# The first norm's modulation weights in four parts instead of two, and the tokens at the head of the load queue

## The chip, the cores and the metric

The kernel runs on one core of one Trainium2 chip. The metric is the device time of one execution in microseconds (us), the median of three runs. A core has five engines that run side by side and meet through semaphores: TensorE (PE in the profile, with its weight loads shown apart as PEld), VectorE (DVE), ScalarE (ACT), GpSimd (POOL) and SyncE (SP), which here issues nearly all loads. Each engine takes its own instructions in their order.

## The reference, cut to what matters

One block of a diffusion backbone over 512 latent tokens (x) with 256 context tokens (ctx), 1024 features, float32. Only its beginning is touched by the change:

```
mod_lat = jnp.split(jax.nn.silu(c) @ w_ada[l] + b_ada[l], 6, axis=-1)
mod_ctx = jnp.split(jax.nn.silu(c_ctx)[None, :] @ w_ada[l] + b_ada[l], 6, axis=-1)
sh1, sc1, gt1, sh2, sc2, gt2 = mod_lat
...
pl = project(modulate(rmsnorm(x, g_mix[l]), sh1, sc1), w_in[l], w_dec_up[l], b_dec[l])
pc = project(modulate(rmsnorm(ctx, g_mix[l]), sh1c, sc1c), w_in[l], w_dec_up[l], b_dec[l])
```

The first norm needs a shift and a scale for each feature, from the first 2 x 1024 columns of `w_ada` (8.4 MB). `project` multiplies the modulated tokens by `w_in`; attention, convolution, gates and the channel layer (SwiGLU) follow, and are the same in both kernels.

## The kernel before, in words

Tokens are kept turned, features on the partitions: `h[f]` is feature tile f (128 features x 512 tokens) of the modulated tokens, f = 0 to 7. float32 operands are split into a high and a low half, and a product takes three matmuls (`mm3`: high x high, high x low, low x high).

**Loads.** SP issues the loads in program order: `c_rows` (c and c_ctx, 4 KB each, L167), `vrow` (norm gains and `b_ada`, L180), the four token tiles `xt` (512 KB each, L236), the first half of `w_ada` (`wa`, 8 loads of 512 KB: for each input tile k the 512 shift and 512 scale columns of feature tiles 0 to 3, L272), head 0's weights for input tiles 0 to 3 (`r_w`: two units of two tiles, 557 KB each in four loads, L438), the second half of `w_ada` (16 loads of 256 KB, L266), the other two units of `r_w`, then small vectors and two context tiles. An operand `w_dec_up` (`wraw`) comes over POOL.

**Before the first product.** ACT applies Silu to the turned `c_rows` (`c`), DVE puts the result into `cw`. Each token tile is squared and summed on ACT (`junk`), scaled on DVE (`normed`), turned by PE (`xtp`), and copied into `xsT` by ACT and DVE (`turn`). `ada_rows` multiplies `cw` into `wa` on PE; DVE copies the rows (`adar`); `mod_cols` turns them with a selecting matrix `sel` on PE (`adac`), and DVE adds `b_ada` (`modT`) and the gain (`gs`). `modulate(f)` makes `h[f]`: ACT the high half, DVE the low half (`xsT` in place, then a subtraction). `w0_split` splits a unit of `r_w` into `h_w` (ACT) and `l_w` (DVE).

**Gather.** For k = 0 to 7, `gather_v` multiplies `h[k]` into four banks `v` (12 matmuls), `gather_kq` into `kl` and `q` (3 matmuls each). `ada_rows(1)`, `mod_cols(1)` and the remaining modulates are written at k = 3. After k = 5 the context tiles are turned (`xtp` again) and modulated (`hc`, `mod_ctx`). Then the same gather runs over the context (`v`, `kc` from `hc`), and at its k = 5 PE turns `st` (`ddt`), which ACT and DVE make from the finished `v` banks in `v_done`, after `hc`. `warm` gives PE products of zeros.

From there on PE, DVE, ACT and SP have the same instructions in the same order in both kernels; between the helpers `act_`, `dve`, `mm` and `tr` the written order is kept.

Of the kernel before, what the change touches and what calls it, by code (L numbers as in the profile page):

```python
# [8 lines left out]
F32 = mybir.dt.float32  # L9
# [33 lines left out]
R_GM, R_GF, R_BA, R_GH, R_BD, R_WC, R_N = 0, 8, 16, 64, 66, 74, 98  # L43
# [3 lines left out]
def hybrid_block(ctx: ExitStack, tc: tile.TileContext, x, c, ctxt, c_ctx, w_ada, b_ada, g_mix, w_in,  # L47
                 w_dec_up, b_dec, g_head, w_gla_out, w_conv, w_conv_out, w_mix_out, g_ffn,
                 w_ffn_in, w_ffn_out, g_final, out):
    nc = tc.nc  # L50
    x, ctxt, out = x[0], ctxt[0], out[0]
    w_ada, w_in, w_gla_out, w_conv_out, w_mix_out = (w[0] for w in (w_ada, w_in, w_gla_out, w_conv_out, w_mix_out))
# [3 lines left out]
    wp = ctx.enter_context(tc.tile_pool(name="wp", bufs=3))  # L56
# [8 lines left out]
    def u2(name, dt=F32, shape=(P, 512)):  # L65
        return up.tile(list(shape), dt, tag="u2", name=name, bufs=NU)
# [126 lines left out]
    for d in range(2):  # L193
# [4 lines left out]
        s = 1 if d == 0 else -1  # L198
# [9 lines left out]
    for d in range(2):  # L208
        t = cst.tile([P, NT, P], F32, name=f"TP{d}")
# [7 lines left out]
    root = sm.tile([P, 1], F32, tag="ss", name="root")  # L217
    nc.scalar.activation(root, c2[:, 0:1], AF.Sqrt, bias=eps, scale=0.0)
    c2v = c2.rearrange("p (s k) -> p k s", s=2)
    hp = tc.alloc_tile_pool(name="hp", bufs=1)  # L220

    cw = u2("cw", F32, (P, KT, 32))
    nc.vector.memset(cw, 0.0)
    nc.vector.tensor_copy(cw[:, :, 0:2], c2v)

    sel = hp.tile([P, 2, 2], F32, name="sel")
    for s_ in range(2):
        nc.vector.tensor_add(sel[:, s_, :], ident[:, 32 * s_:32 * s_ + 2], ident[:, 64 + 32 * s_:66 + 32 * s_])
# [4 lines left out]
    def token_load(i):
        if i < NT:
            xt = hp.tile([P, D], F32, tag="xt", name=f"xt{i}", bufs=4)
            nc.sync.dma_start(xt, x[i * P:(i + 1) * P, :])  # L236
        else:
            xt = wp.tile([P, D], F32, tag="raw", name=f"xt{i}", bufs=4)
            nc.sync.dma_start(xt, ctxt[(i - NT) * P:(i - NT + 1) * P, :])
        return xt  # L240
# [14 lines left out]
    modT = cst.tile([P, KT, 2, 2], F32, name="modT")  # L255
    gs = cst.tile([P, KT, 2], F32, name="gs")

    def ada_load(hf):

        us = []  # L260
        for k in range(KT):
            src = w_ada[k * P:(k + 1) * P, :2 * D].rearrange("p (s f) -> p s f", s=2)[:, :, hf * 512:(hf + 1) * 512]
            if hf == 1:
                ts = [(uo if s_ else uh)(f"wa{k}{s_}") for s_ in range(2)]
                for s_ in range(2):
                    nc.sync.dma_start(ts[s_], src[:, s_, :])  # L266
            else:
                if k % 2 == 0:
                    t = wp.tile([P, 2, 512], F32, tag="raw", name=f"wa0{k}", bufs=4)
                else:  # L270
                    t = hp.tile([P, 2, 512], F32, tag="wa", name=f"wa0{k}", bufs=4)
                nc.sync.dma_start(t, src)  # L272
                ts = [t[:, s_, :] for s_ in range(2)]
            us.append(ts)
        return us

    def ada_rows(hf, us):

        rows = gbank(f"ada{hf}")
        for k in range(KT):  # L280
            for s_ in range(2):
                g_ = 64 * (k % 2) + 32 * s_
                mm(rows[g_:g_ + 32, :], cw[:, k, :], us[k][s_], start=k < 2, stop=k >= KT - 2)
        rsb = u2(f"adar{hf}")
        dve.tensor_copy(rsb, rows)
        return rsb

# [7 lines left out]
        dve.tensor_scalar(src, src, g_, sh, ALU.mult, ALU.add)  # L295
        dve.tensor_sub(lo, src, f32(hi))

    def mod_cols(hf, rsb):
        cp = gbank(f"adac{hf}")
        for i in range(4):  # L300
            mm(cp[:, 4 * i:4 * i + 4], rsb[:, i * P:(i + 1) * P], sel.rearrange("p s c -> p (s c)"), start=True, stop=True)
        fs = slice(4 * hf, 4 * hf + 4)
        ba = vec[:, R_BA:R_BA + 2 * KT].rearrange("p (s f) -> p f s", s=2)
        dve.tensor_tensor(modT[:, fs], cp[:, 0:16].rearrange("p (f s c) -> p f s c", f=4, s=2),
                          ba[:, fs, :].unsqueeze(3).broadcast_to([P, 4, 2, 2]), ALU.add)

        dve.scalar_tensor_tensor(gs[:, fs, :], modT[:, fs, 1, :], 1.0,
                                 vec[:, R_GM + 4 * hf:R_GM + 4 * hf + 4].unsqueeze(2).broadcast_to([P, 4, 2]), ALU.add, ALU.mult)

    def modulate(f):  # L310
        mod_split(xsT[:, f, :], f, 0, *h[f])
# [136 lines left out]
    def gather(o, c0, src, k, n=T):  # L448
        mm3(o[:, :n], w0_at(k, c0, c0 + P), tuple(w_[:, :n] for w_ in src[k]), k == 0, k == KT - 1)
# [3 lines left out]
    def warm(n):  # L453

        for _ in range(n):
            mm(vo[0], zeros[:, :P], zeros, start=True, stop=True)

    vo = [bank(f"v0_{NC_}")]

    wdu_ = wdu_load()  # L460
    xts = [token_load(i) for i in range(NT)]
    was = [ada_load(0)]
    wrs = [w0_load(p_) for p_ in range(2)]
    was.append(ada_load(1))
    wrs += [w0_load(p_) for p_ in range(2, 4)]
    small_vectors(((R_GH, g_head), (R_BD, b_dec[0]), (R_WC, w_conv[0])))
    xcs = [token_load(NT + i) for i in range(NC_)]
    lat = (xsT[:, :4, :], xsT[:, 4:, :])
    pinned[0] = True
    vps = bank("vps")  # L470
    tr(vps[:, :64], vrow[:64, :P], ident[:64, :64])
    dve.tensor_copy(vec[:, :64], vps[:, :64])
    normed(0, xts[0])
    for i in range(NT):
        if i + 1 < NT:
            normed(i + 1, xts[i + 1])
        turn(i, xts[i], lat, i)
    wdu_split(*wdu_)
    rsb = ada_rows(0, was[0])
    mod_cols(0, rsb)  # L480
    warm(9)

    def w0_split(p_):
        w0.append(split_raw(wrs[p_], f"w0{p_}"))

    modulate(0)
    w0_split(0)
    for f in range(1, 4):
# [431 lines left out]
    for pr in range(KT // 2):  # L920
# [77 lines left out]
    for t in range(NT):  # L998
        xt = [uo(f"x1_{t}{i}") for i in range(2)]
# [193 lines left out]
```

## Time and profile before

| | |
|---|---|
| median of 3 runs (lowest, highest) | 1011.58 us (1011.58, 1013.21) |
| profiled execution | 1012.35 us |
| its span, first to last instruction | 1010.6 us |
| PE busy | 986.5 us (98%) |
| DVE / ACT busy | 543.3 us (54%) / 382.1 us (38%) |
| loads and stores | 117.16 MB |

The profile is of one execution. Times in it count from the start of the span; some 1.75 us of the execution lie outside it. A row of the timeline names its engine, the line of the kernel (L102, L148 and L151 are the helpers through which most instructions pass), the operation and `output<-inputs` by tile name, with the idle time before it and what ended that in brackets.

### The profile page before, as it was taken

To read this page: it belongs to the slowest core of one execution; us is meant where nothing else is said; L and a number is where in the kernel's file an instruction comes from. 1 tells how busy PE (TensorE), PEld (TensorE's weight loads), DVE (VectorE), ACT (ScalarE), POOL (GpSimd) and SP (SyncE) were. 2 spreads that over 40 slices of the span, in tenths; PEclk is the share of its full clock that TensorE was granted. 3 is DMA by queue.
4 is the path that set the end of the run, shared out by engine and by line. 5 is a ranking of instruction groups with operands and counts; after the bars stand their busy time and mean duration, and the time that the engine had idled before them with its cause. 6 is when DMAs were issued, how large, how long until landed. Compare 5 with 4: busy or idle time off the path is not lost.

```text
span 1010.6 us, 12827 instructions
## 1 busy us (share of the span) xinstructions
PE 986.5 (98%) x5204; PEld 823.4 (81%) x5204; DVE 543.3 (54%) x838; ACT 382.1 (38%) x602; POOL 6.4 (1%) x18
## 2 busy tenths in 40 slices
PE   5899999999999999999999999999999999999997
PEld 2688888888788888888888888988888888888886
DVE  5577876766556777767543345643323333423424
ACT  4457465559345223224222324632322323311313
POOL 2000000000000000000000000000000000000000
PEclk9999999999999999999999999999999999999999
DMA  8742212112337676666533222242332332331302
GB/s 297 262 118 59 65 33 64 30 55 48 119 104 208 198 210 187 176 189 216 155 94 98 84 84 84 85 125 84 104 104 84 104 104 84 106 123 63 125 21 84
DMA packets 105535, 117.16 MB, mean 116 GB/s; under 512 B 5394, under 2 KB 89476, under 8 KB 105476
## 3 DMA queue, kind: packets, MB, share of 16 engines
q1 hardware_dynamic: 105220, 116.07, 37.6%
q8 instruction: 41, 0.67, 0.3%
q0 software_dynamic: 256, 0.26, 0.1%
q14 instruction: 18, 0.15, 0.0%
HBM read 114.22 MB, written 2.10 MB: 115 GB/s over the span
## 4 chain that ended last, share of the span: by engine, by line
PE 93%; DMA 2%; ACT 2%; DVE 2%; issue 0%; SPq 0%; ACTq 0%; DVEq 0%
PE f L148 24%; PE fo L148 11%; PE v L148 6%; PE yc L148 4%; PE yg L148 4%; PE gb L148 4%; PE cb L148 4%; PE g L148 4%; PE ch L148 4%; PE cc L148 4%; PE ga L148 4%; PE mx L148 3%; PE kl L148 2%; PE q L148 2%; PE o L148 2%; PE F L148 2%
## 5 line engine op out<-in xcount | busy, mean ns | idle before, releaser
L148 PE MATMUL f<-h,h_fa 128*128 128x512 f32 (+1 forms) x384 | 111.1, 372 | 0.2 <-DVE h L102 0.2
L148 PE MATMUL f<-h,h_fb 128*128 128x512 f32 (+1 forms) x384 | 110.3, 372 | 0.0
L148 PEld LDWEIGHTS f<-h,h_fa 128*128 128x128 f32 x384 | 70.2, 188 | 13.4 <-DVE h L102 0.8
L148 PEld LDWEIGHTS f<-h,h_fb 128*128 128x128 f32 x384 | 70.0, 188 | 12.5
L148 PE MATMUL f<-h,l_fb 128*128 128x512 f32 (+1 forms) x192 | 71.3, 371 | 0.0
L148 PE MATMUL f<-h,l_fa 128*128 128x512 f32 (+1 forms) x192 | 71.3, 371 | 0.0
L102 DVE TENSOR_TENSOR l_fa<-r_fa,h_fa 128x1024 fp32r<-128x1024 f32 x22 | 26.9, 1225 | 74.6 <-ACT h_fa L102 74.6
L102 DVE TENSOR_TENSOR l_fo<-r_fo,h_fo 128x1024 fp32r<-128x1024 f32 x22 | 26.8, 1224 | 68.7 <-ACT h_fo L102 68.7
L148 PE MATMUL fo<-h_fo,ah 128*128 128x512 f32 x154 | 60.5, 393 | 0.0
L148 PE MATMUL fo<-l_fo,ah 128*128 128x512 f32 x154 | 60.5, 393 | 0.0
L148 PE MATMUL fo<-h_fo,al 128*128 128x512 f32 x154 | 60.4, 392 | 0.0
L910 DVE SCALAR_TENSOR_TENSOR acc<-r_wa,c,acc 128x256 f32<-128x256 f32 x112 | 54.1, 483 | 8.8 <-DMA r_wa<-in_w_ada_dram 6.1
L102 ACT CAST h_fo<-r_fo 128x1024 fp32r<-128x1024 f32 x22 | 23.1, 1050 | 71.0 <-PE fo L148 27.4
L148 PEld LDWEIGHTS f<-h,l_fb 128*128 128x128 f32 x192 | 36.2, 188 | 6.2
L148 PEld LDWEIGHTS f<-h,l_fa 128*128 128x128 f32 x192 | 36.1, 188 | 6.2
L148 PE MATMUL gb<-h,h_gb 128*128 128x512 f32 x128 | 40.0, 394 | 0.0
L148 PE MATMUL g<-h,h_g 128*128 128x512 f32 x128 | 39.7, 392 | 0.0
L148 PE MATMUL cb<-h,h_cb 128*128 128x512 f32 x128 | 39.7, 391 | 0.0
L148 PE MATMUL cc<-h,h_cc 128*128 128x512 f32 x128 | 39.6, 390 | 0.0
L148 PE MATMUL ch<-h,h_ch 128*128 128x512 f32 x128 | 39.5, 390 | 0.0
L148 PE MATMUL ga<-h,h_ga 128*128 128x512 f32 x128 | 39.5, 390 | 0.0
L1125 DVE TENSOR_TENSOR sil<-sil,f 128x512 f32<-128x512 f32 x22 | 15.1, 687 | 39.5 <-PE f L148 39.5
(297 smaller groups left out, 2275.9 us busy)
## 6 DMA issues: line engine op xcount, KB each, us to landing
r_wa<-in_w_ada_dram SPq DMA_DIRECT2D x32, 512.0 KB, 4.7
r_fa<-in_w_ffn_in_dram SPq DMA_DIRECT2D x22, 512.0 KB, 3.5
r_fb<-in_w_ffn_in_dram SPq DMA_DIRECT2D x22, 512.0 KB
r_fo<-in_w_ffn_out_dram SPq DMA_DIRECT2D x22, 512.0 KB, 3.5
wa<-in_w_ada_dram SPq DMA_DIRECT2D x8, 512.0 KB, 12.1
wa<-in_w_ada_dram SPq DMA_DIRECT2D x16, 256.0 KB, 5.7
r_g<-in_w_in_dram SPq DMA_DIRECT2D x8, 512.0 KB, 3.9
r_gb<-in_w_in_dram SPq DMA_DIRECT2D x8, 512.0 KB
```

What stands on the lines that cost most here:

```text
L102: return lambda *a, **k: pin(getattr(self.engine, op)(*a, **k))
L148: pe_pin(nc.tensor.matmul(*a, **k))
L910: nc.vector.scalar_tensor_tensor(acc, w_[:, k, :], ck, acc, ALU.mult, ALU.add)
L1125: nc.vector.tensor_mul(sil, sil, obs[2 + j])
```

## The change

`w_ada`'s first 2 x 1024 columns come in four parts of two feature tiles each (256 shift and 256 scale columns; 8 loads of 256 KB a part), and after each part the unit of `r_w` with the same two input tiles. A part's product with `cw` is one matmul per k of 512 columns, shift and scale side by side (before: one for each). `ada_rows`, `mod_cols`, two modulates and one `w0_split` are done part by part within the gather, at k = 1, 3 and 5. The four token tiles are loaded ahead of `c_rows` and `vrow`. The `vps` turn of `vrow` and `wdu_split` (five DVE instructions) move behind the token tiles; the context is turned after k = 6 instead of k = 5. In `mod_cols` the selected column pairs, modT and gs have half the width, four times instead of twice.

```diff
--- before.py
+++ after.py
@@ -163,6 +163,18 @@
...
+    xts = [token_load(i) for i in range(NT)]
     c_rows = cst.tile([16, P], F32, name="c_rows")
     nc.sync.dma_start(c_rows[0:8, :], c.rearrange("o (r f) -> (o r) f", f=P))
     nc.sync.dma_start(c_rows[8:16, :], c_ctx.rearrange("(r f) -> r f", f=P))
@@ -217,27 +229,18 @@
...
-    sel = hp.tile([P, 2, 2], F32, name="sel")
-    for s_ in range(2):
-        nc.vector.tensor_add(sel[:, s_, :], ident[:, 32 * s_:32 * s_ + 2], ident[:, 64 + 32 * s_:66 + 32 * s_])
+    sel = hp.tile([P, 2], F32, name="sel")
+    nc.vector.tensor_add(sel, ident[:, 0:2], ident[:, 32:34])
+    for g_ in (64, 96):
+        nc.vector.tensor_add(sel, sel, ident[:, g_:g_ + 2])
...
@@ -255,33 +258,33 @@
-    def ada_load(hf):
+    def ada_load(p_):
 
         us = []
+        src = w_ada[:, :2 * D].rearrange("(k p) (s f) -> p k s f", p=P, s=2)[:, :, :, p_ * 256:(p_ + 1) * 256]
+        if p_ < 2:
+            for k in range(0, KT, 2):
+                if p_ == 0:
+                    t = wp.tile([P, 2, 2, 256], F32, tag="raw", name=f"wa{p_}{k}", bufs=4)
+                else:
+                    t = hp.tile([P, 2, 2, 256], F32, tag="wa", name=f"wa{p_}{k}", bufs=4)
+                for i in range(2):
+                    nc.sync.dma_start(t[:, i], src[:, k + i])
+                us += [t[:, i].rearrange("p s f -> p (s f)") for i in range(2)]
+        else:
+            for k in range(KT):
+                t = (uh if p_ == 2 else uo)(f"wa{p_}{k}", F32, (P, 2, 256))
+                nc.sync.dma_start(t, src[:, k])
+                us.append(t.rearrange("p s f -> p (s f)"))
+        return us
+
+    def ada_rows(p_, us):
+
+        rows = gbank(f"ada{p_}")
         for k in range(KT):
-            src = w_ada[k * P:(k + 1) * P, :2 * D].rearrange("p (s f) -> p s f", s=2)[:, :, hf * 512:(hf + 1) * 512]
...
-        for k in range(KT):
-            for s_ in range(2):
-                g_ = 64 * (k % 2) + 32 * s_
-                mm(rows[g_:g_ + 32, :], cw[:, k, :], us[k][s_], start=k < 2, stop=k >= KT - 2)
-        rsb = u2(f"adar{hf}")
+            g_ = 32 * (k % 4)
+            mm(rows[g_:g_ + 32, :], cw[:, k, :], us[k], start=k < 4, stop=k >= KT - 4)
+        rsb = u2(f"adar{p_}")
         dve.tensor_copy(rsb, rows)
         return rsb
...
@@ -458,36 +461,34 @@
     wdu_ = wdu_load()
-    xts = [token_load(i) for i in range(NT)]
-    was = [ada_load(0)]
-    wrs = [w0_load(p_) for p_ in range(2)]
-    was.append(ada_load(1))
-    wrs += [w0_load(p_) for p_ in range(2, 4)]
+    was, wrs = [], []
+    for p_ in range(4):
+        was.append(ada_load(p_))
+        wrs.append(w0_load(p_))
...
-    vps = bank("vps")
-    tr(vps[:, :64], vrow[:64, :P], ident[:64, :64])
-    dve.tensor_copy(vec[:, :64], vps[:, :64])
     normed(0, xts[0])
     for i in range(NT):
         if i + 1 < NT:
             normed(i + 1, xts[i + 1])
         turn(i, xts[i], lat, i)
-    wdu_split(*wdu_)
+    vps = bank("vps")
+    tr(vps[:, :64], vrow[:64, :P], ident[:64, :64])
+    dve.tensor_copy(vec[:, :64], vps[:, :64])
     rsb = ada_rows(0, was[0])
+    warm(4)
     mod_cols(0, rsb)
-    warm(9)
+    warm(6)
 
     def w0_split(p_):
         w0.append(split_raw(wrs[p_], f"w0{p_}"))
 
     modulate(0)
     w0_split(0)
-    for f in range(1, 4):
-        modulate(f)
-    w0_split(1)
+    modulate(1)
+    wdu_split(*wdu_)
...
@@ -501,24 +502,22 @@
     for k in range(KT):
-        if k == 3:
-            rsb = ada_rows(1, was[1])
+        p_ = k // 2 + 1
+        more = k % 2 == 1 and p_ < 4
         gather_v(vo, h, k)
-        if k == 2:
-            continue
-        if k == 3:
-            mod_cols(1, rsb)
-            gather_kq(2)
-            modulate(4)
-            w0_split(2)
-            modulate(5)
-            modulate(6)
-            w0_split(3)
-            modulate(7)
-            for i in range(NC_):
-                normed(NT + i, xcs[i])
-        gather_kq(k)
-        if k == 5:
+        if more:
+            rsb = ada_rows(p_, was[p_])
+            gather_kq(k - 1)
+            mod_cols(p_, rsb)
+            modulate(2 * p_)
+            w0_split(p_)
+            modulate(2 * p_ + 1)
+            if p_ == 3:
+                for i in range(NC_):
+                    normed(NT + i, xcs[i])
+        if k % 2 or k >= 6:
+            gather_kq(k)
+        if k == 6:
             xcT = [wp.tile([P, 4, TC], F32, tag="raw", name=f"xcT{i}", bufs=4) for i in range(2)]
```

On SP, the head of the queue in program order. Before:

```order
L167 DMA c_rows<-in_c_dram 8x128
L168 DMA c_rows<-in_c_ctx_dram 8x128
L180 DMA vrow<-in_g_mix_dram 8x128
L180 DMA vrow<-in_g_ffn_dram 8x128
L180 DMA vrow<-in_b_ada_dram 48x128
L236 DMA xt_150<-in_x_dram 128x1024
L236 DMA xt_152<-in_x_dram 128x1024
```

On SP, the same place of the changed kernel:

```order
L171 DMA xt_73<-in_x_dram 128x1024
L171 DMA xt_75<-in_x_dram 128x1024
L171 DMA xt_77<-in_x_dram 128x1024
L171 DMA xt_79<-in_x_dram 128x1024
L179 DMA c_rows<-in_c_dram 8x128
L180 DMA c_rows<-in_c_ctx_dram 8x128
L192 DMA vrow<-in_g_mix_dram 8x128
```

The four token tiles now stand ahead of the two loads of `c_rows`.

On PE, where the gather passes from one set of modulated features to the next (h, k and q of the third and fourth input tile, adac, then the first product with the next `h_w`). Before, from the second half's adac on:

```order
L148 MATMUL adac_459<-sel,adar_445 128x4 x4
L148 MATMUL kl_378<-h_131,h_w_371 128x512
L148 MATMUL kl_378<-h_133,h_w_371 128x512
L148 MATMUL kl_378<-h_131,l_w_372 128x512
L148 MATMUL q_379<-h_131,h_w_371 128x512
L148 MATMUL q_379<-h_133,h_w_371 128x512
L148 MATMUL q_379<-h_131,l_w_372 128x512
L148 MATMUL kl_378<-h_131,h_w_371 128x512
L148 MATMUL kl_378<-h_133,h_w_371 128x512
L148 MATMUL kl_378<-h_131,l_w_372 128x512
L148 MATMUL q_379<-h_131,h_w_371 128x512
L148 MATMUL q_379<-h_133,h_w_371 128x512
```

On PE in the changed kernel, at the passage from the first part to the second (the other two read alike):

```order
L148 MATMUL q_371<-h_140,h_w_355 128x512
L148 MATMUL q_371<-h_142,h_w_355 128x512
L148 MATMUL q_371<-h_140,l_w_356 128x512
L148 MATMUL adac_413<-sel,adar_405 128x2 x4
L148 MATMUL kl_370<-h_140,h_w_355 128x512
L148 MATMUL kl_370<-h_142,h_w_355 128x512
L148 MATMUL kl_370<-h_140,l_w_356 128x512
L148 MATMUL q_371<-h_140,h_w_355 128x512
L148 MATMUL q_371<-h_142,h_w_355 128x512
L148 MATMUL q_371<-h_140,l_w_356 128x512
L148 MATMUL v_2_148<-h_w_423,h_140 128x288
L148 MATMUL v_2_148<-l_w_424,h_140 128x288
```

Before, two tiles' kl and q (12 matmuls) stand between adac and the next `v`; now one tile's (6 matmuls) do, and the other tile's stand ahead of adac.

On PE, the turn of the context tiles. Before (`h_w_475` is the third unit of head 0's weights, `h_w_485` the fourth):

```order
L148 MATMUL q_379<-h_132,l_w_476 128x512
L151 MATMUL xtp_0_550<-ident,xt_232 128x128 x4
L151 MATMUL xtp_1_556<-ident,xt_232 128x128 x4
L151 MATMUL xtp_0_562<-ident,xt_234 128x128 x4
L151 MATMUL xtp_1_568<-ident,xt_234 128x128 x4
L148 MATMUL v_2_139<-h_w_485,h_132 128x288
```

On PE in the changed kernel, where `h_w_551` is the fourth unit:

```order
L148 MATMUL q_371<-h_141,l_w_552 128x512
L151 MATMUL xtp_0_598<-ident,xt_241 128x128 x4
L151 MATMUL xtp_1_604<-ident,xt_241 128x128 x4
L151 MATMUL xtp_0_610<-ident,xt_243 128x128 x4
L151 MATMUL xtp_1_616<-ident,xt_243 128x128 x4
L148 MATMUL v_2_148<-h_w_551,h_141 128x288
```

The turn has moved one input tile later: one tile of the gather (k = 7) is left behind it instead of two.

## Rows read from the trace of the kernel before

**Rows 1.** Windows: busy us (instructions) of each engine, granted clock, DMA share, GB/s.

```profile
0.00:30.70 30.70, 16.66 (x84) 8.50 (x84) 16.32 (x45) 14.11 (x25) 6.44 (x18) 1.00 0.91 302
30.70:76.00 45.30, 43.62 (x291) 37.10 (x291) 29.68 (x60) 21.47 (x46) 0.00 (x0) 1.00 0.57 174
76.00:1010.60 934.60, 926.21 (x4833) 777.85 (x4829) 497.26 (x734) 346.57 (x532) 0.00 (x0) 1.00 0.35 107
```

**Rows 2.** Chain that ended last, first 30 us: start us, us, what.

```profile
4.51 9.92 DMA wa<-in_w_ada_dram
14.45 10.23 DMA r_w<-in_w_in_dram
```

**Rows 3.** Timeline of SP, first loads: start us, us, instruction.

```profile
0.81 0.40 SPq L167 DMA_DIRECT2D c_rows<-in_c_dram  x1
2.62 1.84 SPq L236 DMA_DIRECT2D xt<-in_x_dram  x4
```

**Rows 4.** Timeline of ACT, the start.

```profile
4.61 0.29 ACT L218 ACTIVATE root<-c,eps 128x1 f32<-128x1 f32 x1
7.33 1.06 ACT L102 ACTIVATE junk<-xt 128x1024 bf16<-128x1024 f32 x1 [2.42 <-DMA xt<-in_x_dram]
```

**Rows 5.** Timeline of PE, up to the gather's start.

```profile
2.82 0.26 PE L214 MATMUL cps<-ident,c_rows 16*128 16x16 f32 x1 [2.82 <-DMA c_rows<-in_c_ctx_dram]
...
9.85 3.67 PE L151 MATMUL xtp<-ident,xt 128*128 128x128 f32 x16 [5.51 <-DVE xt L102]
...
15.94 1.06 PE L151 MATMUL xtp<-ident,xt 128*128 128x128 f32 x8 [0.68 <-DVE xt L102]
...
23.85 1.05 PE L148 MATMUL ada<-wa,cw 128*32 128x512 f32 x4 [0.31 <-DMA wa<-in_w_ada_dram]
...
30.70 0.40 PE L148 MATMUL v<-l_w,h 128*128 128x288 f32 x1 [1.12 <-DVE l_w L102]
```

**Rows 6.** The turning products' times on PE, windows 10.8 to 12 and 15.9 to 17.

```profile
L151 PE MATMUL xtp<-ident,xt x7: 417/417/417, 10.5 to 11.8; 128*128 128x128 f32 x7
L151 PE MATMUL xtp<-ident,xt x8: 272/273/301, 15.9 to 16.7; 128*128 128x128 f32 x8
```

**Rows 7.** Timeline of PE, the gather.

```profile
38.29 3.64 PE L148 MATMUL ada<-wa,cw 128*32 128x512 f32 x32
...
43.56 0.95 PE L148 MATMUL adac<-sel,adar 128*128 128x4 f32 x8
...
48.34 0.40 PE L148 MATMUL v<-l_w,h 128*128 128x288 f32 x1 [0.84 <-DVE l_w L102]
...
51.28 0.29 PE L148 MATMUL v<-h_w,h 128*128 128x288 f32 x1
...
52.88 0.63 PE L148 MATMUL kl<-h,h_w 128*128 128x512 f32 x2
...
54.26 1.04 PE L151 MATMUL xtp<-ident,xt 128*128 128x128 f32 x8
...
56.49 0.38 PE L148 MATMUL v<-h_w,h 128*128 128x288 f32 x1
...
62.55 0.29 PE L148 MATMUL v<-h_w,hc 128*128 128x288 f32 x1
...
69.61 0.38 PE L148 MATMUL v<-h_w,hc 128*128 128x288 f32 x1
```

**Rows 8.** Timeline of DVE.

```profile
19.65 0.69 DVE L102 TENSOR_TENSOR wdu<-wraw,wdhi 32x512 fp32r<-32x512 f32 x1
...
24.95 0.69 DVE L102 COPY adar<-ada 128x512 f32<-128x512 f32 x1 [4.61 <-PE ada L148]
...
44.55 0.17 DVE L102 TENSOR_TENSOR modT<-adac,vec 128x16 f32<-128x16 f32 x1 [1.78 <-PE adac L148]
...
63.43 0.42 DVE L102 TENSOR_TENSOR hc<-xcT,hc 128x256 fp32r<-128x256 f32 x1
...
68.81 0.23 DVE L102 TENSOR_TENSOR st<-v,ddh 128x64 f32<-128x64 f32 x1 [0.25 <-ACT ddh L102]
```

More of the change, by code (lines that the diff above doesn't have):

```diff
@@ L163, in rstd_of, with token_load @@
         return r
+    hp = tc.alloc_tile_pool(name="hp", bufs=1)
+    def token_load(i):
+        if i < NT:
+            xt = hp.tile([P, D], F32, tag="xt", name=f"xt{i}", bufs=4)
+            nc.sync.dma_start(xt, x[i * P:(i + 1) * P, :])
+        else:
+            xt = wp.tile([P, D], F32, tag="raw", name=f"xt{i}", bufs=4)
+            nc.sync.dma_start(xt, ctxt[(i - NT) * P:(i - NT + 1) * P, :])
+        return xt
+    xts = [token_load(i) for i in range(NT)]
     c_rows = cst.tile([16, P], F32, name="c_rows")
@@ L219, in hybrid_block @@
     c2v = c2.rearrange("p (s k) -> p k s", s=2)
-    hp = tc.alloc_tile_pool(name="hp", bufs=1)
     cw = u2("cw", F32, (P, KT, 32))
@@ L224, in hybrid_block @@
     nc.vector.tensor_copy(cw[:, :, 0:2], c2v)
-    sel = hp.tile([P, 2, 2], F32, name="sel")
-    for s_ in range(2):
-        nc.vector.tensor_add(sel[:, s_, :], ident[:, 32 * s_:32 * s_ + 2], ident[:, 64 + 32 * s_:66 + 32 * s_])
+    sel = hp.tile([P, 2], F32, name="sel")
+    nc.vector.tensor_add(sel, ident[:, 0:2], ident[:, 32:34])
+    for g_ in (64, 96):
+        nc.vector.tensor_add(sel, sel, ident[:, g_:g_ + 2])
     xsT = hp.tile([P, KT, T], F32, name="xsT")
[L233 to L240, printed above, removed]
     def normed(i, xt):
@@ L256, in hybrid_block @@
     gs = cst.tile([P, KT, 2], F32, name="gs")
-    def ada_load(hf):
+    def ada_load(p_):
         us = []
-        for k in range(KT):
-            src = w_ada[k * P:(k + 1) * P, :2 * D].rearrange("p (s f) -> p s f", s=2)[:, :, hf * 512:(hf + 1) * 512]
-            if hf == 1:
-                ts = [(uo if s_ else uh)(f"wa{k}{s_}") for s_ in range(2)]
-                for s_ in range(2):
[L266 to L279, printed above, removed]
-        for k in range(KT):
-            for s_ in range(2):
-                g_ = 64 * (k % 2) + 32 * s_
-                mm(rows[g_:g_ + 32, :], cw[:, k, :], us[k][s_], start=k < 2, stop=k >= KT - 2)
-        rsb = u2(f"adar{hf}")
+        src = w_ada[:, :2 * D].rearrange("(k p) (s f) -> p k s f", p=P, s=2)[:, :, :, p_ * 256:(p_ + 1) * 256]
[8 more added lines that the diff above has]
+                us += [t[:, i].rearrange("p s f -> p (s f)") for i in range(2)]
+        else:
+            for k in range(KT):
[5 more added lines that the diff above has]
+        rows = gbank(f"ada{p_}")
+        for k in range(KT):
+            g_ = 32 * (k % 4)
+            mm(rows[g_:g_ + 32, :], cw[:, k, :], us[k], start=k < 4, stop=k >= KT - 4)
+        rsb = u2(f"adar{p_}")
         dve.tensor_copy(rsb, rows)
@@ L296, in mod_split, with mod_cols @@
         dve.tensor_sub(lo, src, f32(hi))
-    def mod_cols(hf, rsb):
-        cp = gbank(f"adac{hf}")
+    def mod_cols(p_, rsb):
+        cp = gbank(f"adac{p_}")
         for i in range(4):
-            mm(cp[:, 4 * i:4 * i + 4], rsb[:, i * P:(i + 1) * P], sel.rearrange("p s c -> p (s c)"), start=True, stop=True)
-        fs = slice(4 * hf, 4 * hf + 4)
+            mm(cp[:, 2 * i:2 * i + 2], rsb[:, i * P:(i + 1) * P], sel, start=True, stop=True)
+        fs = slice(2 * p_, 2 * p_ + 2)
         ba = vec[:, R_BA:R_BA + 2 * KT].rearrange("p (s f) -> p f s", s=2)
-        dve.tensor_tensor(modT[:, fs], cp[:, 0:16].rearrange("p (f s c) -> p f s c", f=4, s=2),
-                          ba[:, fs, :].unsqueeze(3).broadcast_to([P, 4, 2, 2]), ALU.add)
+        dve.tensor_tensor(modT[:, fs], cp[:, 0:8].rearrange("p (s f c) -> p f s c", f=2, s=2),
+                          ba[:, fs, :].unsqueeze(3).broadcast_to([P, 2, 2, 2]), ALU.add)
         dve.scalar_tensor_tensor(gs[:, fs, :], modT[:, fs, 1, :], 1.0,
-                                 vec[:, R_GM + 4 * hf:R_GM + 4 * hf + 4].unsqueeze(2).broadcast_to([P, 4, 2]), ALU.add, ALU.mult)
+                                 vec[:, R_GM + 2 * p_:R_GM + 2 * p_ + 2].unsqueeze(2).broadcast_to([P, 2, 2]), ALU.add, ALU.mult)
     def modulate(f):
```

## The prediction

> **What bounds the kernel now.** I read three views in turn. The busy time by windows comes first [rows 1]: after 76 us PE is idle for 934.60 - 926.21 = 8.4 us in 935, so the rest of the kernel is PE's own work, which the change does not touch. PE is idle for 14.0 of the first 30.7 us, and loads run at 302 GB/s there. Whatever the change does, it does before 76 us, and from there on the time moves as PE's front moves. The chain that ended last comes second [rows 2]: the front hangs on loads, `wa` for 9.9 us and then `r_w` for 10.2 us. The timelines come third. They give the moment from which PE works without a longer break: 30.70, when the low half `l_w` of head 0's first weights is ready [rows 5], and the moment at which the latent gather is done and the context's begins: 62.55 [rows 7]. Between them lie 31.85 us. I work out both numbers for the changed kernel, and then what happens right behind.
>
> **The start: tokens first.** Before, `c_rows` is issued at 0.81 [rows 3] and used by PE at 2.82 [rows 5], 2.0 us later. The first token tile is issued at 2.62 and used at 7.33 [rows 3, 4], 4.71 us later. Issued at 0.81 it lands at 5.52. Three more tiles of 512 KB follow; loads of that size land 0.31 + 1.05 = 1.36 us apart (`wa` [rows 5]), so the last lands at 9.60. Now `c_rows` lies behind them. Does it wait for them? The row on `r_w` says yes: a load of 262 KB, issued behind `wa`, took 10.2 us [rows 2]. So `c_rows` lands at 9.6. The Trainium skill's page "DMA: Bandwidth & Descriptors" has two rules that pull apart here: by "Queues, rings and completion order" an engine consumes descriptors in ring order, which is what that row shows; by the fit in "Anatomy of one DMA — SWDGE (gpsimd) path", written for GpSimd's loads, a load costs 2.0 us plus its bytes over 436 GB/s, by which `c_rows` would land near 5 us. I take the first; the second is a rival.
>
> This matters because Silu of `c_rows` and `root` stand on ACT ahead of the first token's squares. From the use of `c_rows` to the end of `root` went 4.61 + 0.29 - 2.82 = 2.08 us [rows 4, 5]. So the first square starts at 9.60 + 2.08 = 11.7 instead of 7.33: 4.35 us later, although the token has been there since 5.5. What follows on ACT, DVE and PE is the same chain for four tiles, which waited for no load after the first square; the turns ended at 15.94 + 1.06 = 17.0 [rows 5] and now end at 21.35. The moved `vps` turn adds one product, 0.27 us at the later turns' 272 ns [rows 6]. Part 0 of `w_ada` is there by then: 2.1 MB behind 9.60 is four times 1.36 us, 15.0. Its product is half of the second half's 3.64 us [rows 7], 1.82, so `adar` starts at 23.5. From `adar` to the gather's 30.70 went 30.70 - 24.95 = 5.75 us [rows 5, 8]; `warm(4)` ahead of adac lies beside DVE's copy of `adar`. The gather starts at 29.25: **1.45 us earlier** than before, not the 5.4 us (four times 1.36) that 2.1 MB less of `w_ada` ahead of it would give.
>
> Bounds: if `c_rows` slips past the tokens, it lands 2.0 us after an issue at about 3.0 (estimate: four tiles at 1.84 in all, then one more load [rows 3]), the square starts at 7.1 and the gather at 24.7. The latest it can land is when the `wa` load behind the tokens did, 4.51 + 9.92 = 14.43 [rows 2], less the 1.81 us by which the queue now starts earlier and the 1.36 of that load itself: 11.3, and the gather starts at 30.9.
>
> **The gather: four parts.** PE passes from one set of features to the next like this: adac, then modT, gs, ACT's high half of `h`, DVE's low half, and `l_w`, then the first products. From adac to modT went 44.55 - 43.56 = 0.99, from modT to the first product with `l_w` 48.34 - 44.55 = 3.79 us [rows 7, 8]. A narrower modT can save less than the 0.17 us it took [rows 8]; I count nothing. Before, two tiles' kl and q stood behind adac: 2 x 1.38 (52.88 to 54.26 [rows 7]) = 2.76 us of cover, and PE still stood for 0.84. Now one tile's 1.38 us cover it, and it happens three times. A part therefore takes two tiles' v (1.60 each, 51.28 to 52.88), the rows 1.82, one kl and q 1.38, adac 0.99, and the chain 3.79, under which the other kl and q lie: **11.18 us**, of which some 2.3 us are standing still. The `adar` copy (0.69 [rows 8]) lies under the first kl and q. `wdu_split`, five DVE instructions of at most 0.69 us [rows 8], lies under the first part's v and rows (5.0 us); without that cover it would cost up to 3.4 us once. Loads are not what is waited for: part 3 is read at 29.25 + 2 x 11.18 + 3.2 = 54.8, and all of x, `w_ada` and `r_w` (2.2 MB) lands by 9.6 + 16 x 1.36 + 4.3 x 1.36 = 37; even if the shorter runs of 1 KB cost a quarter of the rate on `w_ada`, 44. SP keeps ahead of them: it issues 12 loads a part, at 1.84 / 4 = 0.46 us each [rows 3] 5.5 us, where a part's 2.66 MB take 6.9. `sel`'s two further additions run on DVE while it waits for the first token.
>
> Three parts take 33.5 us. Behind them come k = 6 (2.98, 51.28 to 54.26), the context's turn (2.23, 54.26 to 56.49) and k = 7 (half of 62.55 - 56.49, 3.03): 8.24 us. The sum is 41.8 where it was 31.85: **9.9 us more**. By kind: standing still 3 x 2.3 - 0.9 = 6.0, rows 3 x 1.82 - 3.64 = 1.8, adac twice more, 2 x 0.99 = 2.0.
>
> **Behind the gather: the later turn.** DVE modulates the context after its turn, then makes `st`; PE turns `st` (`ddt`) and goes on at 69.61. From the end of the turn to that went 69.61 - 56.49 = 13.12 us. It is DVE's pace, not PE's: `hc` runs until 63.85 and the last `st` until 69.04 [rows 8], right ahead of 69.61. PE had 62.55 to 69.61 = 7.06 us of work there behind two tiles' 6.06. Now it has one tile's 3.03 ahead, 10.09 in all, and stands for **3.0 us** at `ddt`. The bounds are 0, if DVE gains on it, and 3.0: before, both arrived together, so I take 3.0.
>
> **Sum.** -1.45 + 9.9 + 3.0 = +11.5 us. Against the profiled execution (1012.35) that is 1023.85; it stood 0.77 above the median of the runs shown, so against 1011.58 I predict **1023.1 us**.
>
> **Rivals.** (a) `c_rows` slips past the tokens: the gather starts 6.0 us earlier than before, the sum is -6.0 + 9.9 + 3.0 = +6.9, 1018.5 us. For it: it did land in 2.0 us when nothing was ahead. Against it: `r_w`'s 10.2 us.
>
> (b) TensorE's clock falls while PE stands. Its turning products took 417 ns at 10.5 to 11.8, after 5.51 us without work [rows 5], and 272 at 15.9 [rows 6], while the granted clock reads 1.00 in all three windows [rows 1]. If the three stands of 2.3 us do the same, each is followed by some 4 us of work at 417/272 of its time, about 1.4 to 2 us lost: +4 to 6, 1028 us. Against it: the stands before (up to 1.12 us [rows 5]) left no trace, and the new ones are shorter than 5.5.
>
> (c) PE does not stand: it takes later products past the one that waits. That would spare 3 x 2.3 at the passages and 3.0 at `ddt`, 9.9 of the 11.5 us, and leave 1013.2, which is no change; it decides from about 9.5 us on. Against it: at 48.34 PE stood for 0.84 us [rows 7] although products with `h_w` alone, whose data were there, came next. The Trainium skill's page "TensorE: Matmul & The Clock Gate", section "Packing small matmuls: row/col tiling", has matmuls in strict order and only weight loads pulled ahead; the trace agrees with its 0.84 us.
>
> **How the numbers follow.** The forecast has 0.78, (a) 0.09, (b) 0.06, (c) 0.03, and 0.04 is left for what I do not see. A gain would need a start at 17.8, before the last token can have been turned in any of these cases. The forecast's own bounds are a `c_rows` at 11.3 (+1.65, 1024.8) and a `ddt` that costs half (1021.6). The range reaches to (a) and leaves (b) out: 1018 to 1025. What a measurement of this kernel can tell from no change is about 0.2%, 2 us. Slower: the forecast, (a), (b) and part of the rest, 0.94; same 0.04; faster 0.02.
>
> **What would show it.** In the profile after: the first square on ACT near 11.7 (7.1 under (a)), with ACT waiting for Silu's input; the first product with `l_w` near 29.3; three waits of PE for `l_w` of about 2.3 us, 11.2 us apart; no wait of the rows for `wa` at parts 1 to 3; the context's gather from about 71; a wait at `ddt` of about 3 us; and nothing new after that. It would be wrong if PE's waits at the passages were under 1 us, if the gather began before 24, or if products behind a passage took half again their time.

## The result and the profile after

The changed kernel takes **1027.86 us** (median; 1026.94 to 1028.95), the kernel before 1011.63 us on the same chip: 1.6% slower, ratio 1.0157 with a 95% interval of 1.0139 to 1.0175. The prediction was 1023.1 us with a range of 1018 to 1025. The sign and the steps of the sum came out as forecast; the time lies outside the range, at the 1028 of rival (b).

The profiled execution took 1028.95 us, its span 1027.2: 16.6 us more than before. The first view is again the windows: the stages (start, latent gather, context gather up to the product `z` that follows the last `ddt`, the rest), and between them stretches of 3 us from within the gather. The columns are those of [rows 1].

```profile
0.00:29.32 29.32, 12.30 (x69) 8.06 (x70) 14.14 (x41) 13.14 (x23) 6.27 (x18) 1.00 1.02 309
29.32:76.25 46.93, 40.96 (x231) 31.73 (x232) 22.49 (x43) 14.12 (x23) 0.00 (x0) 0.89 0.41 124
76.25:92.31 16.06, 12.98 (x89) 11.62 (x87) 11.92 (x29) 8.29 (x25) 0.00 (x0) 1.00 0.49 136
92.31:1027.20 934.89, 926.51 (x4833) 778.19 (x4833) 497.14 (x734) 346.34 (x532) 0.00 (x0) 1.00 0.36 107
...
30.00:33.00 3.00, 3.00 (x14) 3.00 (x14) 2.93 (x6) 0.00 (x0) 0.00 (x0) 0.50 1.13 328
...
43.00:46.00 3.00, 3.00 (x16) 3.00 (x15) 0.34 (x1) 0.00 (x0) 0.00 (x0) 0.54 0.57 176
...
53.00:56.00 3.00, 1.30 (x8) 1.09 (x8) 2.93 (x5) 1.24 (x2) 0.00 (x0) 1.00 0.00 0
56.00:59.00 3.00, 3.00 (x27) 2.46 (x29) 0.23 (x1) 0.00 (x0) 0.00 (x0) 1.00 0.02 5
...
67.00:70.00 3.00, 3.00 (x12) 2.72 (x12) 2.25 (x5) 1.30 (x3) 0.00 (x0) 0.52 0.01 3
```

The last stage, 934.89 us with PE busy for 926.51, reads as before: the whole difference lies ahead of `z`. In the gather PE is idle for 6 of 47 us, and the granted clock, 1.00 everywhere before [rows 1], is 0.89. The 3 us stretches show where: three times it stands at 0.5, the lower of its two levels (1.2 GHz), while PE is busy without a break. Each time PE had just waited: the first fall lies behind the opening waits, of which the last, 1.12 us ahead of 29.32, was there before as well [rows 5]; the other two lie behind the first and the third of the three passages. From 53 to 59 us, at the second passage, the same waits are followed by no fall.

The timeline of ACT at the start, where before the first square ran at 7.33 [rows 4]:

```profile
10.03 0.18 ACT L228 ACTIVATE c<-cps 128x16 f32<-128x16 f32 x1 [7.95 <-PE cps L226]
...
11.53 0.29 ACT L230 ACTIVATE root<-c,eps 128x1 f32<-128x1 f32 x1
11.73 1.04 ACT L102 ACTIVATE junk<-xt 128x1024 bf16<-128x1024 f32 x1
```

The timeline of PE, answering to [rows 5, 7]:

```profile
9.74 0.25 PE L226 MATMUL cps<-ident,c_rows 16*128 16x16 f32 x1 [9.74 <-DMA c_rows<-in_c_ctx_dram]
...
21.52 1.92 PE L148 MATMUL ada<-wa,cw 128*32 128x512 f32 x16
...
29.32 0.41 PE L148 MATMUL v<-l_w,h 128*128 128x288 f32 x1 [1.12 <-DVE l_w L102]
...
30.25 0.68 PE L148 MATMUL v<-h_w,h 128*128 128x288 f32 x2
...
33.08 0.43 PE L148 MATMUL v<-h_w,h 128*128 128x288 f32 x2
...
40.69 0.40 PE L148 MATMUL v<-h_w,h 128*128 128x288 f32 x1 [0.78 <-ACT h_w L102]
42.21 0.40 PE L148 MATMUL v<-l_w,h 128*128 128x288 f32 x1 [1.13 <-DVE l_w L102]
...
55.10 0.40 PE L148 MATMUL v<-l_w,h 128*128 128x288 f32 x1 [1.13 <-DVE l_w L102]
...
61.69 0.95 PE L148 MATMUL adac<-sel,adar 128*128 128x2 f32 x8
...
66.46 0.40 PE L148 MATMUL v<-l_w,h 128*128 128x288 f32 x1 [1.13 <-DVE l_w L102]
...
76.25 0.29 PE L148 MATMUL v<-h_w,hc 128*128 128x288 f32 x1
...
83.38 0.30 PE L151 MATMUL ddt<-ident,st 128*128 128x128 f32 x1 [0.68 <-ACT st L102]
84.61 0.30 PE L151 MATMUL ddt<-ident,st 128*128 128x128 f32 x1 [0.93 <-ACT st L102]
85.83 0.30 PE L151 MATMUL ddt<-ident,st 128*128 128x128 f32 x1 [0.92 <-ACT st L102]
...
92.31 0.62 PE L148 MATMUL z<-ddT,wdu 64*128 64x256 f32 x4 [0.52 <-DVE ddT L102]
```

Read by stages, with before in [rows 5, 7] and this row of before's PE timeline for `z`:

```profile
75.69 0.62 PE L148 MATMUL z<-ddT,wdu 64*128 64x256 f32 x4 [0.52 <-DVE ddT L102]
```

| | before | after | difference | forecast |
|---|---|---|---|---|
| start, to the first `v` with `l_w` | 30.70 | 29.32 | -1.38 | -1.45 |
| latent gather, to the first `v` with `hc` | 31.85 | 46.93 | +15.08 | +9.9 |
| context gather, to `z` | 13.14 | 16.06 | +2.92 | +3.0 |
| sum | 75.69 | 92.31 | +16.62 | +11.5 |

Two terms hit within 0.1 us. The gather is 5.2 us over. Its parts, from one `l_w` product to the next, take 42.21 - 29.32 = 12.89, 12.89 and 66.46 - 55.10 = 11.36 us, where 11.18 was forecast. The two long parts are those with a stretch at 0.5; the third fall (67 to 70) lies behind the last passage, in a tail of 76.25 - 66.46 = 9.79 us where 8.24 was forecast. So a fall costs 12.89 - 11.36 = **1.53 us**. Three falls are 4.6, three parts of 0.18 are 0.5, together 5.1.

`z` is a good mark: the execution's time less its `z` is 936.66 us before and 936.64 after, and between 936.63 and 936.72 in the profiled executions of all the experiments. What a variant gains or loses, it does ahead of `z`.

### The profile page after: what moved, and what is told of

Its sections match the earlier page's. It is cut to its first block, busy times and chain, and to the rows that moved or that the text cites. A ratio compares the mean times of both kernels' runs of the same rounds, so it can differ in the third digit from the quotient of the medians.

```text
span 1027.2 us, 12874 instructions
## 1 busy us (share of the span) xinstructions
PE 992.8 (97%) x5221; PEld 829.6 (81%) x5221; DVE 545.7 (53%) x845; ACT 381.9 (37%) x602; POOL 6.3 (1%) x18
## 4 chain that ended last, share of the span: by engine, by line
PE 91%; DMA 3%; DVE 3%; ACT 2%; SPq 1%; issue 1%; ACTq 0%; DVEq 0%
PE f L148 23%; PE fo L148 10%; PE v L148 6%; PE yc L148 4%; PE yg L148 4%; PE gb L148 4%; PE cb L148 4%; PE g L148 4%; PE cc L148 4%; PE ch L148 4%; PE ga L148 4%; PE mx L148 3%; PE kl L148 2%; PE o L148 2%; PE q L148 2%; PE F L148 2%
## 5 line engine op out<-in xcount | busy, mean ns | idle before, releaser
L148 PE MATMUL v<-h_v,h 128*128 128x256 f32 x192 | 36.3, 285 | 0.0
```

## The experiments

The theory: the kernel lost 11 to 12 us by the steps of the forecast (start by `c_rows`, three stands, more rows and adac, `ddt`), and the rest by falls of the clock behind PE's waits. The rival: the start, the stands or the clock are not the cause, and the gap comes from the products or the loads of the four parts. Executions of one such kernel differ in how many falls they have; medians and profiled executions are therefore told apart. Times of before on the same chip were 1011.5 to 1011.6 us beside every run but the two at which 1012.35 is given.

**The small loads ahead of the tokens.** Only the order on SP is put back:

```diff
-    xts = [token_load(i) for i in range(NT)]
     c_rows = cst.tile([16, P], F32, name="c_rows")
...
     small_vectors(((R_GM, g_mix), (R_GF, g_ffn), (R_BA, b_ada)))
+    xts = [token_load(i) for i in range(NT)]
```

> The changed kernel with the two loads of c_rows and the three of vrow ahead of the token tiles again, as before the change; nothing else differs. Theory (the tokens' chain waits for Silu of c_rows, which lands behind 2 MB of tokens): the first square goes from 11.7 back to about 7.3 us, part 0 of w_ada becomes the limit (it landed fourth of its kind at 18.4 in the kernel before), the first product with l_w comes at 24.7 instead of 29.3, and the time is 4.6 us shorter, about 1023.3. Rival (the start is set by the transfers whatever leads the queue): the start moves by less than 1 us and so does the time.

Measured 1023.26 us (1023.11 to 1024.58), 4.6 less than after. PE's timeline:

```profile
2.81 0.25 PE L226 MATMUL cps<-ident,c_rows 16*128 16x16 f32 x1 [2.81 <-DMA c_rows<-in_c_ctx_dram]
...
16.37 2.96 PE L148 MATMUL ada<-wa,cw 128*32 128x512 f32 x16
...
25.10 0.40 PE L148 MATMUL v<-l_w,h 128*128 128x288 f32 x1 [1.12 <-DVE l_w L102]
```

The gather starts 4.22 us earlier than in after. Now the loads of `w_ada` pace its rows (2.96 against 1.92 us). So with the smaller first part the gather starts 30.70 - 25.10 = 5.6 us earlier than before (5.4 by the forecast's loads), and putting the tokens first gave 4.2 of them back. The median is as expected in part by luck: `z` comes at 86.58, 5.7 us earlier than in after's profiled execution, 1.5 of it because this one has two falls (behind the first and the third passage) and none behind the opening waits.

**Tokens first in the kernel before.** The reverse, with the `vps` turn behind the tokens as in the change:

```diff
+    xts = [token_load(i) for i in range(NT)]
     c_rows = cst.tile([16, P], F32, name="c_rows")
...
-    xts = [token_load(i) for i in range(NT)]
```

> The kernel before with only its tokens ahead of c_rows and vrow, and the turn of vrow behind the tokens. Theory (the start is the later of two chains, the tokens' behind c_rows, and w_ada): c_rows lands near 9.6 and the turns end 4.35 us later, at 21.4, but the first half of w_ada was the limit with 23.9 us and still ends at about the same time, so the first product with l_w moves by 0.4 us or less: 1012.0, no change that can be measured. Rival (putting the tokens first costs 4 to 5 us in any kernel): 1016.

Measured 1012.37 us (1012.21 to 1014.07), ratio 1.0009 (1.0000 to 1.0018). PE's timeline:

```profile
9.25 0.26 PE L226 MATMUL cps<-ident,c_rows 16*128 16x16 f32 x1 [9.25 <-DMA c_rows<-in_c_ctx_dram]
...
21.03 3.64 PE L148 MATMUL ada<-wa,cw 128*32 128x512 f32 x32
...
30.48 0.40 PE L148 MATMUL v<-l_w,h 128*128 128x288 f32 x1 [1.12 <-DVE l_w L102]
```

Here the late `c_rows` costs little, 0.8 us in the medians, since the rows waited for `wa` before [rows 5] and now wait for nothing. Only together with the smaller first part does the token order cost 4.2 us. This execution (1013.61) has one fall behind the opening wait, so a kernel with the gather of before is not free of them either; a window of it:

```profile
31.00:35.00 4.00, 4.00 (x17) 3.41 (x16) 3.93 (x6) 1.03 (x2) 0.00 (x0) 0.58 1.06 387
```

**Zeros in the stands.** PE multiplies zeros while it would stand, at the passages into a bank of their own (the second argument of `warm`); no wait is removed.

```diff
-    warm(6)
+    warm(16)
...
             gather_kq(k)
+        if more:
+            warm(9, gbank(f"zb{p_}"))
```

> The changed kernel with nine products of zeros (bf16, 512 columns, into a bank of their own) in each of the three stands at the passages, and ten more ahead of the first gather; all other work is the same. Theory (TensorE's clock falls after the stands and takes 1.7 us each time): the granted clock stays 1.00 throughout, the v products keep 0.29 us, and the time is about 5 us shorter, 1022.8, although PE does more. Rival (the slow products have another cause, such as a crowded PSUM or SBUF): the slow products stay, and the time is the same or up to 0.6 us longer for the products of zeros.

Measured 1025.72 us (1025.3 to 1025.86): 2.1 less, not 5. PE's timeline at the first passage, then windows:

```profile
38.14 2.12 PE L148 MATMUL zb<-zeros 128*128 128x512 bf16 x8
...
40.61 0.40 PE L148 MATMUL v<-l_w,h 128*128 128x288 f32 x1 [0.22 <-DVE l_w L102]
```

```profile
17.00:82.00 65.00, 59.34 (x376) 42.38 (x380) 37.60 (x77) 25.39 (x50) 0.00 (x0) 1.00 0.59 175
82.00:86.00 4.00, 4.00 (x22) 4.00 (x21) 3.18 (x6) 1.98 (x5) 0.00 (x0) 0.58 0.31 89
```

All three parts take 11.36 us, and the clock holds through the gather. But it now falls once behind the waits at `ddt`, where it had held in after: about 1.5 us given back.

**Zeros at `ddt` too**, 3, 4 and 4 of them between its turning products.

```diff
             tr(tp[:, (i - a) * P:(i - a + 1) * P], stv[i // 4][:, i % 4, :], ident)
+            if a and i < e - 1:
+                warm(3 if i == a else 4, zb)
```

> The kernel after with zero products in the three stands at the passages (as in the run before with zeros) and also in the three waits for st at the ddt turn (3, 4 and 4 of 0.22 us in waits of 0.67, 0.93 and 0.92 us), in a bank of their own. They take no wait away; they only keep PE busy in it. If the forecast's sum was right and only the falls of the granted clock were left out of it, there is now no stretch at 0.5 between 18 us and the z products, z comes 1.5 us earlier than with zeros in the stands alone (89.13), near 87.6, and the median is 1023.2 us, within 0.5 us of the forecast 1023.1, with its executions close together. Rival: the zeros cost what they give, or the cost lies elsewhere: 1025.7 as with zeros in the stands alone.

Measured 1024.65 us (1024.42 to 1025.53), ratio 1.0122 (1.0108 to 1.0136), with before at 1012.35: 12.3 us slower than before, where after was 16.2. PE's timeline and the window of the whole gather:

```profile
10.18 0.26 PE L226 MATMUL cps<-ident,c_rows 16*128 16x16 f32 x1 [10.18 <-DMA c_rows<-in_c_ctx_dram]
...
29.76 0.40 PE L148 MATMUL v<-l_w,h 128*128 128x288 f32 x1 [0.27 <-DVE l_w L102]
...
88.12 0.62 PE L148 MATMUL z<-ddT,wdu 64*128 64x256 f32 x4 [0.52 <-DVE ddT L102]
```

```profile
17.00:92.00 75.00, 72.39 (x445) 51.95 (x444) 44.92 (x91) 32.12 (x65) 0.00 (x0) 1.00 0.57 169
```

Without a fall, `z` comes 88.12 - 75.69 = 12.4 us later than before; 0.4 of that is a `c_rows` that landed 0.44 us later than in after. That leaves 12.0, against 11.5 forecast. From the first `l_w` product to `z` it is 58.36 us, in after 62.99: 4.63 less, three falls of 1.54.

**The turn of the context back behind k = 5**, and its norms at k = 4:

```diff
+        if k == 4:
+            for i in range(NC_):
+                normed(NT + i, xcs[i])
...
-        if k == 6:
+        if k == 5:
             xcT = [wp.tile([P, 4, TC], F32, tag="raw", name=f"xcT{i}", bufs=4) for i in range(2)]
```

> The changed kernel with the context's turn after k = 5 again (and its tokens normed at k = 4, so that the turn does not wait for them). Theory (DVE needs some 13 us from the turn to the last st, and one tile of the gather less stands ahead of ddt): PE's wait of 2.5 to 3 us at ddt goes, the turn costs up to 0.7 us more because its last two products wait for copies behind the modulation of tile 7, and the time is about 2.3 us shorter, 1025.6. Rival (the wait at ddt is only moved to the next place that needs DVE): no change within 0.5 us.

Measured 1024.24 us (1022.1 to 1025.38), 3.6 less. PE's timeline:

```profile
66.25 0.66 PE L151 MATMUL xtp<-ident,xt 128*128 128x128 f32 x4 [1.10 <-ACT xcT L102]
67.58 1.02 PE L151 MATMUL xtp<-ident,xt 128*128 128x128 f32 x4 [0.68 <-ACT xcT L102]
...
81.77 0.60 PE L151 MATMUL ddt<-ident,st 128*128 128x128 f32 x4
```

`ddt` waits for nothing, and from its first product to `z` it is 88.46 - 81.77 = 6.69 us, in after 9.88. The turn now stands where the third passage stood: the waits there are gone, and two new ones (1.78 us) take the place of 0.78 and 1.13, so that the turn does not cost the 0.7 us allowed for it. Hence more than expected. The three falls stay, the third now behind the waits of the turn.

**Two tiles' kl and q behind adac**, as before the change, with the rows ahead of the second v:

```diff
-        gather_v(vo, h, k)
         if more:
             rsb = ada_rows(p_, was[p_])
-            gather_kq(k - 1)
+        gather_v(vo, h, k)
+        if more:
             mod_cols(p_, rsb)
+            gather_kq(k - 1)
```

> The changed kernel with each part's rows ahead of the second v of a pair and both tiles' kl and q behind adac, as the kernel before had it at its one passage. Theory (the stand is the 3.8 us from modT to l_w less what covers it, and the clock falls only after the longer stands): each stand goes from 2.3 to 0.9 us, 4.1 us in all, and the falls of the clock, worth 5.1 us, go too: 9.2 us shorter, 1018.7. Rival 1 (any stand brings the clock down): 4.1 us shorter with the slow products still there. Rival 2 (the stands are not set by cover): less than 1 us.

Measured 1022.63 us (1021.81 to 1025.0), 5.2 less. The wait is 0.83 us at each passage, as the 0.84 of [rows 7], and the parts take 9.97 us. The context's first `kc` comes at 69.53 instead of 78.62, 9.1 us earlier (0.3 of it because `c_rows` landed earlier) where the theory had 9.2: in this execution no fall comes at the passages. But the clock falls at the `ddt` waits (0.71, 0.93 and 0.90 us), this time for longer, which takes back some 2.5 us of it (from `kc` to `z` 16.15 us instead of 13.69). Whether stands of 0.83 us never bring a fall is not shown: the executions differ by 3.2 us, and only one was profiled. The window of the fall at `ddt`:

```profile
75.00:82.00 7.00, 5.55 (x23) 5.18 (x24) 4.58 (x9) 4.01 (x11) 0.00 (x0) 0.55 0.21 59
```

**The split of head 0's weights right behind the rows**, ahead of kl, q and adac, so that `l_w` no longer ends the chain:

```diff
             rsb = ada_rows(p_, was[p_])
+            w0_split(p_)
             gather_kq(k - 1)
             mod_cols(p_, rsb)
             modulate(2 * p_)
-            w0_split(p_)
```

> The changed kernel with parts 1 to 3 of head 0's weights split right behind the rows of their part, ahead of adac, instead of behind the modulation of the part's first tile. Theory (the stand at a passage is the DVE chain behind modT, in which l_w stands last): l_w drops out of the chain, which ends with the low half of h 2.55 us behind modT instead of 3.79, 1.24 us less three times, and the stands of 1 us that are left do not bring the clock down at the passages (5.1 us): the context's gather starts some 8.8 us earlier, near 67.5. The wait at ddt stays and may bring the clock down there, as in the runs with zeros and with two covers (1.5 to 2.5 us lost): 1019 to 1021.5. Rival (PE waits at the passages for ACT's half or for loads): less than 1 us.

Measured 1022.09 us (1020.26 to 1024.1), 0.6 above the expected range. The profiled execution is the fastest and has the context's gather at 67.54, as expected; its window of the gather, and PE's wait at the second passage:

```profile
17.00:92.00 75.00, 65.87 (x414) 50.27 (x413) 47.24 (x92) 35.97 (x67) 0.00 (x0) 1.00 0.58 172
```

```profile
49.39 0.53 PE L148 MATMUL v<-h_w,h 128*128 128x288 f32 x2 [0.78 <-DVE h L102]
```

The stand is one wait of 0.78 us for the low half of `h`; no fall. The mean granted clock of the four executions goes with their time: 0.998 at 1020.26 us, 0.997 at 1021.36, 0.995 at 1022.81, 0.994 at 1024.1.

**The early split with zeros**, 4 at each passage and those at `ddt`. The edit is the sum of those above.

> The kernel with the early split (1022.09 us, its executions between 1020.26 and 1024.1, the profiled one the fastest and without any fall), with 4 zero products in each shorter stand and with zeros at the ddt turn. If its spread is nothing but falls that come in some executions, they go: median near 1020.3, executions within 0.5 us. Rival: 1022, spread as before. In both cases slower than the kernel before (1011.6) by the 3 shorter stands (3 x 1.2), the rows 1.8, adac 2.0 and ddt 2.5 to 3.0 less the start 1.45, so about 8.5.

Measured 1021.03 us (1019.92 to 1021.2), with before at 1012.35. The spread of 3.8 us is down to 1.3, four of five executions within 0.2, and the mean clock is 0.998 or 0.999 in all five. The profiled execution (1021.03) misses 1020.3 because `c_rows` landed at 10.47 in it, 0.84 later than in the early split's (9.63). So the spread of the early split did come from falls.

**All of it in one kernel**: small loads first, rows ahead of the second v, the early split, both kl and q behind adac, the turn behind k = 5, the context's loads ahead of the last small vectors.

> The four parts kept, with small loads first, the rows ahead of the second v of a pair, weights split early, both kl and q behind adac, the context loaded ahead of the small vectors and turned after k = 5. Theory: the start at 25.1, a part of 8.8 us with nothing left to stand for (v 3.2, rows 1.82, adac 0.99, kl and q 2.76), the context's gather from 60.1 instead of 62.55, no new wait at ddt, no fall of the clock: 1009.2, 0.24% under the kernel before. Rival (four parts cost more than they bring whatever the order): 1012 or more.

Measured 1014.46 us (1012.32 to 1015.44): a miss by 5. PE's timeline of an execution of 1012.56 us:

```profile
25.07 0.40 PE L148 MATMUL v<-l_w,h 128*128 128x288 f32 x1 [1.13 <-DVE l_w L102]
...
26.89 3.38 PE L148 MATMUL ada<-wa,cw 128*32 128x512 f32 x16
...
40.78 0.95 PE L148 MATMUL adac<-sel,adar 128*128 128x2 f32 x8
...
50.69 1.05 PE L148 MATMUL adac<-sel,adar 128*128 128x2 f32 x8 [0.87 <-DVE adar L102]
...
75.92 0.62 PE L148 MATMUL z<-ddT,wdu 64*128 64x256 f32 x4 [0.52 <-DVE ddT L102]
```

One fall behind the opening waits makes 16 row products take 3.38 instead of 1.92 us. The third `adar` stands on DVE behind the context's norm and comes late: 9.91 us between these adac, where the pair before had 8.87. Without these 1.46 and 1.04 us `z` would be at 73.4 (an estimate from these rows), 2.3 ahead of before: the expected gain is there and spent. The slower executions were not profiled. Their mean clocks, 0.994 to 0.997 against 0.996 and 0.997 in the three fastest, speak for more falls in most of them, not in all: that of 1014.46 us reads 0.997.

**The early split in the kernel before**, and nothing else of the change, at its first and third unit:

```diff
     rsb = ada_rows(0, was[0])
+    w0_split(0)
     mod_cols(0, rsb)
...
             rsb = ada_rows(1, was[1])
+            w0_split(2)
```

> The kernel before, in two halves, with head 0's first unit split right behind the first rows and the third unit right behind the second rows. Theory (l_w stands last in both chains): the gather starts 0.9 us earlier and the stand of 0.84 us at k = 4 goes: 1009.9, as good as the four parts with everything mended, so that the parts themselves bring next to nothing. Rival (the four parts bring the earlier start and are needed for a gain): 1011 or more.

Measured **1010.43 us** (1010.25 to 1010.78), ratio 0.9987 (0.9978 to 0.9995): the one kernel here that beats both, by 1.15 us where 1.7 were expected. PE's timeline:

```profile
25.01 1.03 PE L148 MATMUL adac<-sel,adar 128*128 128x4 f32 x8 [0.88 <-DVE adar L102]
...
29.99 0.54 PE L148 MATMUL v<-h_w,h 128*128 128x288 f32 x2 [0.78 <-DVE h L102]
...
42.76 0.95 PE L148 MATMUL adac<-sel,adar 128*128 128x4 f32 x8
...
73.79 0.62 PE L148 MATMUL z<-ddT,wdu 64*128 64x256 f32 x4 [0.52 <-DVE ddT L102]
```

And before, the first adac:

```profile
25.79 1.02 PE L148 MATMUL adac<-sel,adar 128*128 128x4 f32 x8 [0.89 <-DVE adar L102]
```

`z` comes 1.9 us earlier, but 0.78 of that is there at the first adac already, ahead of what the edit can touch: the rows' last `wa` landed earlier than in the profiled execution of before. From the first adac to the second it is 17.75 us, before 17.77 [rows 7], so the start gained nothing of the 0.9 us expected. There DVE finishes `l_w` first and reaches `modT` 2.34 us after adac begins (27.35), before 1.07 (26.86): what the split gave at the end of the chain it took at its head. From the second adac to `z` it is 31.03 us, before 32.13. The wait of 0.84 us for `l_w` [rows 7] is gone, and these 1.1 us are the gain that the medians show.

## Why the prediction was off

**The start: right.** The first square came at 11.73 (forecast 11.7), the first `l_w` product at 29.32 (29.25). `c_rows`, 8 KB behind 2.1 MB on the same queue, was used at 9.74, and the start hangs on it alone: in seven profiled executions with four parts and tokens first it was used between 9.43 and 10.47, and the first `l_w` product followed 19.57 to 19.59 us later in each. The Trainium skill's page "DMA: Bandwidth & Descriptors", section "Queues, rings and completion order", adds to the ring order that the semaphore increment of a transfer lands only behind every earlier write of the same DMA engine; the 9.74 agrees. Rival (a) falls.

**The stands: right in place and size.** From adac to the `l_w` product went 66.46 - 61.69 = 4.77 us (0.99 + 3.79 forecast). It shows as two waits, 0.78 for `h_w` and 1.13 for `l_w`, with one product between; PE passed no product ahead, so rival (c) falls. The 0.18 us a part that were missing lie ahead of adac, between `v`, rows and kl/q. The cover of one tile instead of two is shown as the cause by the run that gives it back: waits of 0.83 us, and parts of 9.97 us instead of 11.36.

**`ddt`: right**: 0.68 + 0.93 + 0.92 us of waits and +2.92 in the stage.

**Where it failed** is the clock: the sum puts the falls behind PE's waits at nothing, and leaves them to rival (b). They cost 4.6 of the 5.1 us by which the sum was short. The price in (b), 1.4 to 2 us a fall, was right (1.53). Its 1028 us in all came out partly by luck, since it put one fall at each of the three passages, where after has two there and the third behind the opening waits, which (b) does not name. The prediction's own last sign of being wrong came too: behind the falls two `v` products take 0.68 us instead of 0.43. (b) got 0.06, on the ground that "the stands before (up to 1.12 us) left no trace, and the new ones are shorter than 5.5", and so lay outside the range. Neither half of that reason bears weight. The clock of one execution was taken for a rule, where executions differ: with the gather of before and the tokens first it did fall behind the same opening waits of 0.40 and 1.12. Before's own executions differ as well: of the 25 measured beside that run 10 read a mean clock of 0.996, the three slowest (1012.97 to 1013.42) among them but the fastest too, and the others 0.998 or 0.999. And the 5.5 us was the one row at hand for a slower product, not a bound below which nothing happens. The zeros show the cause: nothing was taken from the waits, the falls went, and 4.6 us with them in the profiled executions, about 4 in the medians (16.2 against 12.3 over before).

What makes one stand bring a fall and the next, with the same waits, none (53 to 59 us in after) stays open, as does why a fall spared in the gather may come at `ddt` instead.

## What to carry to other kernels

A chain that is cut into more parts pays its latency once a part: before splitting a load for an earlier start, count the cover left at each passage, and take work that needs nothing from the new part (here the weight split) out of the chain first, which alone gained 0.13%. It pays only where it does not delay the chain's head, as it did at the start of the last kernel above. Small operands that open the chain belong ahead of the large loads on their queue wherever that chain, and not the loads, sets the start. Where a forecast adds waits to TensorE, price the clock's fall behind them as a term of the sum with its own chance for each wait, and widen the range to it.

## What was unexpected of the hardware

The granted clock fell to 0.5 for some 3 us behind waits of PE as short as 0.78 and 1.13 us, once for most of 7 us (75 to 82) among three of 0.7 to 0.9, and not at every such place. One such fall cost 1.5 us, the long one some 2.5. The executions of kernels with many stands spread by 2 to 4 us, where before's early split spread by 0.5 in 11 executions, all at a mean clock of 0.998 or 0.999. Mending the waits at one place did not keep the clock up at the next: with the stands filled by zeros, or covered by a second tile, it fell at `ddt`.
